# One-pass products of exact parts for the first layer's memory heads, with a softmax turn that starts two chunks earlier

## The chip, the cores and the metric

The kernel runs on one core of one Trainium2 chip, in one launch. The metric is the device time in microseconds of that core. Before the change, three runs took 2043.17, 2043.19 and 2043.20 us; the median is 2043.19 us.

## The reference, cut to what matters

The reference is a two-layer decoder trunk in fp32: 256 positions, model width 2048. Each layer adds a mixer and a gated convolutional MLP. Layer 0 is the one that the change touches. It makes `z = h @ w_in_a` from the normalized input, uses the first 3072 columns for a gated mixer of 12 heads, and the last 512 as queries of four heads that attend to 256 memory tokens:

```python
def memory_attention(q_m, mem, g_mem, w_mem_kv):
    q = q_m.reshape(B, S, MEM_HEADS, MEM_HEAD_DIM)          # 256 x 4 x 128
    kv = rmsnorm(mem, g_mem) @ w_mem_kv
    k = kv[..., :MEM_W].reshape(B, M, MEM_HEADS, MEM_HEAD_DIM)
    v = kv[..., MEM_W:].reshape(B, M, MEM_HEADS, MEM_HEAD_DIM)
    s = jnp.einsum('bshd,bmhd->bhsm', q, k) * (MEM_HEAD_DIM ** -0.5)
    p = jax.nn.softmax(s, axis=-1)
    return jnp.einsum('bhsm,bmhd->bshd', p, v).reshape(B, S, MEM_W)
...
x = x + jnp.concatenate([main, mo], axis=-1) @ w_out[l]
x = x + conv_ffn(rmsnorm(x, g_ffn[l]), w_ffn_up[l], conv_w[l], conv_b[l], w_ffn_down[l])
```

`main` is the gated mixer's 1536 columns (blocks 0 to 11 of 128), `mo` the memory heads' 512 (blocks 12 to 15). Layer 1 has the same memory attention with its own weights; the change leaves it as it is.

## The kernel before, in words

**A product in three passes.** TensorE takes fp32 data in two ways here. A tile of type F32 is multiplied as it is, and a tile of type F32R holds a value that is exact in a shorter form, which takes one pass. The weights are read as fp32, and `chunk` (line 124) makes two F32R tiles of each: ScalarE writes the rounded high part `whi` (L142, or L147 and L164 with a gain), VectorE writes the rest `wlo` (L143, L148). Activations are held in the same way, high part and low part side by side (`xhl`, `mainhl`, `memhl`). A product is then high by high (L179), high weight by low activation (L180) and low weight by high activation (L182): 256 columns each.

**Chunks, pairs and buffers.** A chunk is 128 x 1024 weights, a load of 512 KB that SyncE issues. `raw`, `whi` and `wlo` have four buffers each. `gemm_fm` (line 186) takes two chunks at a time: first L179 and L180 of both, in the order of the chunks, then L182 of both. One pair is 48 matmuls for a GEMM 512 columns wide. `hooks` are functions that are called after a pair, under the number of either chunk.

**What sets the order.** The whole of `start` (line 432) runs under a manual schedule on TensorE, ScalarE, VectorE and SyncE: each engine takes its instructions in the order in which the code is written. In it, the memory's keys and values of layer 0 are accumulated in four PSUM banks over 16 steps, then comes the GEMM of layer 1's keys (eight chunks, `hooks[0]`) and the one of layer 1's values (eight chunks, `hooks[1]`). Layer 0's results are fetched from PSUM by the hooks of the first: under 0 the column scales `mrt`, under 1 the row of scales `mrb` (a matmul, L428, and a copy, L429), under 2 the values `ev` (L477, ScalarE) and the keys `ek` (L260, VectorE), under 3 to 7 the high and low parts of `xhl` (`operand`, L274 and L275). Outside `start` a scheduler sets the order of ScalarE, VectorE and TensorE; in the last two thirds of layer 0's `w_in_a` GEMM SyncE's order is again that of the code.

**Layer 0's memory heads.** In `layer_a` the queries come from a GEMM of eight chunks (`eq` fetches them as F32 `qm`), and then the gated mixer's first half from three GEMMs, c = 0, 1, 2, of eight chunks each. I call their chunks c0.0 to c2.7. Hooks of these three do the memory heads in passing: scores after chunks c0.2 and c0.4 (two heads each, L545, F32), the softmax, then a turn of the probabilities. `Turn.squares` (L91) transposes 32 x 32 squares on VectorE, eight blocks at a time, into `small`; `Turn.place` puts the squares where they belong by 16 DMAs of 64 KB (L96). `self.pending.ask(..., [0] * 6 + [2] * 8)` hands them out: from the call at c = 1, six chunk loads pass, and behind each of the next eight loads SyncE issues two places. The values follow after chunk c2.5 (`out`, L564, F32). `w_out` then starts with blocks 12 to 15, the memory heads.

Of the kernel before, what the change touches and what calls it, by code (L numbers as in the profile page):

```python
# [20 lines left out]
GH = 12  # L21
GW = GH * 128
MH = 4
MW = 512
# [77 lines left out]
class Kernel:  # L102
# [329 lines left out]
    def start(self):  # L432
        nc, t, tc = self.nc, self.t, self.tc
        self.x = self.ap.tile([P, NB, S], F32, name="xT")
        self.xhl = self.ap.tile([P, NB, 512], F32R, tag="xhl", name=self.uid("xhl"))
        mhl = self.ap.tile([P, NB, 512], F32R, tag="big", name=self.uid("memhl"))
        self.kT = [pool.tile([P, MH, S], F32, name=self.uid("kT")) for pool in (self.mk, self.cp)]
        self.mv = [pool.tile([P, 2, MW], F32, name=self.uid("mv")) for pool in (self.mk, self.cp)]
        self.rt = self.cp.tile([P, 2], F32, name="rt0")
        self.rb = self.tmp(self.cp, [P, S], "rbc", 2)  # L440
        with tc.tile_pool(name="st", bufs=1) as st:
            self.gp = st
            mT = st.tile([P, NB, S], F32, name="memT")
            mrt = st.tile([P, 2], F32, name="mrt")
            mrb = st.tile([P, S], F32, name="mrb")
# [16 lines left out]
            kept = {}  # L462
# [8 lines left out]
                self.row_rstd(kept[name], rb, kept[name + "d"])  # L471

            def ek(l, b, acc):
                self.scaled(self.kT[l][:, b : b + 2, :], acc, mrb)

            def ev(l, tb, acc):
                nc.scalar.activation(self.mv[l][:, tb, :], acc, AF.Copy, scale=mrt[:, tb : tb + 1])  # L477

            m = lambda k: mhl[:, k, :]
            w = t["w_mem_kv"]  # L480
# [8 lines left out]
            mm = nc.tensor.matmul  # L489
# [51 lines left out]
    def memory_scores(self, l, h, q, pool, p):  # L541
        nc = self.nc
        acc = self.psum()
        for sb in range(2):
            nc.tensor.matmul(  # L545
                acc[:, sb * S : (sb + 1) * S], q[:, sb * P : (sb + 1) * P], self.kT[l][:, h, :], start=True, stop=True
            )
# [12 lines left out]
    def memory_out(self, l, h, pT, hl):  # L560
        nc, v = self.nc, self.mv[l]
        o = self.psum()
        for mb in range(2):
            nc.tensor.matmul(o[:, :S], v[:, mb, h * P : (h + 1) * P], pT[:, mb * S : (mb + 1) * S], start=mb == 0, stop=mb == 1)  # L564
        self.split(hl[:, GH + h, :], o[:, :S])


# [93 lines left out]
    def layer_a(self):  # L661
# [4 lines left out]
        with ExitStack() as ctx:  # L666
# [20 lines left out]
            qm = la.tile([P, MH, S], F32, name="qm")  # L687
            wT = la.tile([P, GH, P], F32, name="wT")
            bb = la.tile([P, GH, P], F32, name="bb")

            def spatial_weights():
                nc.sync.dma_start(out=bb, in_=t["b_sp"][0].rearrange("(o g) t -> o g t", o=1).to_broadcast([P, GH, P]))
# [14 lines left out]
                        )  # L707

            def eq(b, acc):
                self.scaled(qm[:, b : b + 2, :], acc, rb)  # L710

            hooks = {1: [spatial_weights], **{4 + i: [lambda i=i: gates(3 * i)] for i in range(4)}}
            self.gemm_fm(self.rows(w, 2 * GW, MW), ks, MH, x, eq, hooks=hooks)

            hl = self.ap.tile([P, NB, 512], F32R, tag="big", name=self.uid("mainhl"))
            pm, small = (la.tile([P, MH * 512], F32, name=name) for name in ("pm", "small"))
            turned = Turn(nc, pm, small, 4 * MH)

            def scores(h):
                view = pm[:, 512 * h : 512 * (h + 1)].rearrange("p (m a c) -> p a m c", m=2, a=2)  # L720
                self.memory_scores(0, h, qm[:, h, :], la, view)

            def out(h):
                self.memory_out(0, h, pm[:, 512 * h : 512 * (h + 1)], hl)

            each = lambda f, *hs: [lambda h=h: f(h) for h in hs]
            mhooks = {2: each(scores, 0, 1), 4: each(scores, 2, 3) + [lambda: turned.squares(0, 8)]}, {0: [lambda: turned.squares(8, 8)]}, {5: each(out, *range(MH))}
            for c in range(3):

                def eu(b, acc):  # L730
                    g = 4 * c + b
                    u = self.tmp(la, [P, 2, S], "u", 2)
                    self.scaled(u, acc, rb)
                    nc.scalar.activation(u, u, AF.Gelu)
                    u4 = u.rearrange("p g (n t) -> p g n t", n=2)
                    v4 = vn[:, :, g * P : (g + 2) * P].rearrange("p n (g t) -> p g n t", g=2)
                    nc.vector.tensor_tensor(u4, u4, v4, ALU.mult)
                    self.split_pair(hl[:, g : g + 2, :], u)

                if c == 1:  # L740
                    self.pending.ask(turned.places(), [0] * 6 + [2] * 8)
                with tc.manual_schedule(engines={mybir.EngineType.SP}) if c else nullcontext():
                    self.gemm_fm(self.rows(w, c * 512, 512), ks, 4, x, eu, hooks=mhooks[c])
            self.w_out(0, hl, [12, 13, 14, 15] + list(range(12)))


    def layer_b(self):
# [346 lines left out]
```

## Time and profile before

| | |
|---|---|
| median of three runs | 2043.19 us (2043.17 to 2043.20) |
| span of the profiled execution | 2041.6 us; its own time is not listed apart |
| TensorE busy | 2032.4 us, 100% of the span, 16200 matmul records |
| VectorE, ScalarE busy | 1359.1 us (67%), 1042.8 us (51%) |
| chain that ended last | TensorE 99% |
| granted TensorE clock | 0.999 of full speed on average |
| HBM read | 387.88 MB, 191 GB/s over the span |

The span runs from the first to the last instruction of the profile; the three runs are 1.6 us longer than it. In the rows below, times are microseconds from the span's start. A row of the engines in order of time gives its start, its length, engine, line, operation, output and inputs, and in brackets the idle time ahead of it with what ended it; rows that follow each other on one line are merged (x16). A matmul's length holds its way through the array, so the distance of starts tells its cost. The profile shows an F32 matmul of 256 columns as two records.

### The profile page before, as it was taken

To read this page: it belongs to the slowest core of one execution; us is meant where nothing else is said; L and a number is where in the kernel's file an instruction comes from. 1 tells how busy PE (TensorE), PEld (TensorE's weight loads), DVE (VectorE), ACT (ScalarE), POOL (GpSimd) and SP (SyncE) were. 2 spreads that over 40 slices of the span, in tenths; PEclk is the share of its full clock that TensorE was granted. 3 is DMA by queue.
4 is the path that set the end of the run, shared out by engine and by line. 5 is a ranking of instruction groups with operands and counts; after the bars stand their busy time and mean duration, and the time that the engine had idled before them with its cause. 6 is when DMAs were issued, how large, how long until landed. Compare 5 with 4: busy or idle time off the path is not lost.

```text
span 2041.6 us, 38976 instructions
## 1 busy us (share of the span) xinstructions
PE 2032.4 (100%) x16200; PEld 1966.1 (96%) x16200; DVE 1359.1 (67%) x1847; ACT 1042.8 (51%) x1351; POOL 94.4 (5%) x125
## 2 busy tenths in 40 slices
PE   9999999999999999999999999999999999999998
PEld 8989999999999999999999999999988999889997
DVE  6866667767556666457689876777655667656675
ACT  6754644555435554345555674455543555434543
POOL 0000013000000000000052001200000000000000
PEclk9999999999999999999999999999999999999999
DMA  8575755666656666566665674578766666666654
GB/s 310 189 227 175 196 182 186 201 192 192 199 189 193 198 195 197 188 196 192 190 196 177 177 153 157 189 207 217 223 197 194 190 201 189 195 196 187 197 186 154
DMA packets 236753, 396.70 MB, mean 194 GB/s; under 512 B 47776, under 2 KB 54304, under 8 KB 236448
## 3 DMA queue, kind: packets, MB, share of 16 engines
q1 hardware_dynamic: 236288, 393.70, 63.4%
q8 instruction: 126, 2.06, 0.4%
q10 hardware_dynamic: 288, 0.52, 0.1%
q14 instruction: 51, 0.42, 0.1%
HBM read 387.88 MB, written 2.10 MB: 191 GB/s over the span
## 4 chain that ended last, share of the span: by engine, by line
PE 99%; DMA 0%; issue 0%; DVE 0%; ACT 0%; POOLq 0%; POOL 0%
PE ps L182 26%; PE ps L179 26%; PE ps L180 26%; PE ps L210 6%; PE ps L212 6%; PE ps L211 6%; DMA raw<-in_w_mem_kv 0%; PE ps L877 0%; PE ps L545 0%; PE ps L564 0%; PE ps L517 0%; PE ps L516 0%; PE ps L519 0%; PE ps L703 0%; PE ps L910 0%; PE ps L879 0%
## 5 line engine op out<-in xcount | busy, mean ns | idle before, releaser
L143 DVE TENSOR_TENSOR wlo<-raw,whi 128x1024 fp32r<-128x1024 f32 (+1 forms) x672 | 819.4, 1236 | 607.0 <-issue 402.1
L142 ACT ACTIVATE whi<-raw 128x1024 fp32r<-128x1024 f32 (+1 forms) x672 | 705.0, 1056 | 790.5 <-PE ps L180 579.2
L179 PE MATMUL ps<-xhl,whi 128*128 128x256 f32 x3264 | 752.1, 277 | 0.0
L180 PE MATMUL ps<-xhl,whi 128*128 128x256 f32 x3264 | 750.2, 276 | 0.0
L179 PEld LDWEIGHTS ps<-xhl,whi 128*128 128x128 f32 x3264 | 612.8, 188 | 0.3
L180 PEld LDWEIGHTS ps<-xhl,whi 128*128 128x128 f32 x3264 | 612.6, 188 | 0.3
L182 PE MATMUL ps<-xhl,wlo 128*128 128x256 f32 x3264 | 403.2, 276 | 0.0
L182 PEld LDWEIGHTS ps<-xhl,wlo 128*128 128x128 f32 x3264 | 385.1, 188 | 0.0
L179 PE MATMUL ps<-h,whi 128*128 128x256 f32 x704 | 161.6, 276 | 0.0
L180 PE MATMUL ps<-h,whi 128*128 128x256 f32 x704 | 161.5, 276 | 0.0
L619 DVE SCALAR_TENSOR_TENSOR c<-a,cT,c 128x255 f32<-128x255 f32 (+1 forms) x352 | 146.5, 480 | 0.0
L211 PE MATMUL ps<-wlo,h 128*128 128x512 f32 (+1 forms) x364 | 139.0, 382 | 0.0
L212 PE MATMUL ps<-whi,h 128*128 128x512 f32 (+1 forms) x364 | 138.7, 382 | 0.0
L210 PE MATMUL ps<-whi,h 128*128 128x512 f32 (+1 forms) x364 | 138.3, 382 | 0.0
L179 PEld LDWEIGHTS ps<-h,whi 128*128 128x128 f32 x704 | 132.0, 188 | 0.0
L180 PEld LDWEIGHTS ps<-h,whi 128*128 128x128 f32 x704 | 131.9, 188 | 0.0
L616 ACT ACTIVATE c<-a,cT 128x256 f32<-128x256 f32 x176 | 91.6, 591 | 77.2 <-DVE a L260 77.2
L179 PE MATMUL ps<-mainhl,whi 128*128 128x256 f32 x512 | 118.2, 277 | 0.0
L180 PE MATMUL ps<-mainhl,whi 128*128 128x256 f32 x512 | 117.8, 277 | 0.0
L179 PEld LDWEIGHTS ps<-mainhl,whi 128*128 128x128 f32 x512 | 95.9, 188 | 0.1
L180 PEld LDWEIGHTS ps<-mainhl,whi 128*128 128x128 f32 x512 | 95.8, 188 | 0.1
L182 PE MATMUL ps<-h,wlo 128*128 128x256 f32 x704 | 86.9, 276 | 0.0
(250 smaller groups left out, 1963.2 us busy)
## 6 DMA issues: line engine op xcount, KB each, us to landing
raw<-in_w_ffn_up SPq DMA_DIRECT2D x352, 512.0 KB, 4.2
raw<-in_w_ffn_down SPq DMA_DIRECT2D x176, 512.0 KB, 4.8
raw<-in_w_out SPq DMA_DIRECT2D x64, 512.0 KB, 4.9
raw<-in_w_in_a SPq DMA_DIRECT2D x56, 512.0 KB, 4.4
raw<-in_w_mem_kv SPq DMA_DIRECT2D x30, 512.0 KB, 5.0
raw<-in_w_in_b SPq DMA_DIRECT2D x16, 512.0 KB, 4.5
raw<-in_w_uq SPq DMA_DIRECT2D x12, 384.0 KB, 3.5
raw<-in_w_kv_a SPq DMA_DIRECT2D x8, 512.0 KB, 3.8
```

The source lines that it names most:

```text
L142: nc.scalar.activation(hi[:, :n], raw[:, :n], AF.Copy)
L143: nc.vector.tensor_tensor(lo[:, :n], raw[:, :n], hi[:, :n].bitcast(F32), ALU.subtract)
L179: mm(acc, wh, x[:, :S], start=first, stop=False)
L180: mm(acc, wh, x[:, S:], start=False, stop=False)
L182: mm(acc, wl, x[:, :S], start=False, stop=last)
L210: mm(acc, xh, wh, start=first, stop=False)
L211: mm(acc, xh, wl, start=False, stop=False)
L212: mm(acc, xl, wh, start=False, stop=last)
L616: nc.scalar.activation(c[:, i, :], a[:, i, :], AF.Identity, scale=w(2), bias=w(3))
L619: nc.vector.scalar_tensor_tensor(o, a[:, i, : S - 2 + j], w(j), o, ALU.mult, ALU.add)
```

## The change

- Layer 0's keys `kT[0]` and values `mv[0]` are held as F32R high and low parts. `ek` and `ev` write them for l = 0: `ek` scales the keys into a single fp32 buffer `k0` (VectorE, L260) and splits that (`split_pair`: ScalarE L269, VectorE L270), twice; `ev` writes the high part on ScalarE (L487) and the rest on VectorE (L488). Both still stand under hook 2 of layer 1's key GEMM.
- The queries `qm` are split in the same way by `eq`.
- A score product of 128 queries by 256 keys becomes three F32R matmuls in place of one F32 matmul, and so does each value product.
- `places` are asked with `[0] * 4 + [2] * 8`: two chunks earlier. After chunk c2.3 `parts` makes the high and low parts of the turned probabilities (two ScalarE and two VectorE operations of 128 x 1024), and `out` moves from after chunk c2.5 to after chunk c2.7.
- `w_out` takes the memory heads' blocks 12 to 15 after blocks 0 to 7.
- Tiles share buffers: `turned` is first the spatial weights `wT`, then the probabilities `pm`; `square` is first `bb`, then `small`, then the probabilities' high part; `qm`'s buffer later holds their low part.

```diff
@@ start
-        self.kT = [pool.tile([P, MH, S], F32, name=self.uid("kT")) for pool in (self.mk, self.cp)]
-        self.mv = [pool.tile([P, 2, MW], F32, name=self.uid("mv")) for pool in (self.mk, self.cp)]
+        self.kT = [self.mk.tile([P, MH, 2 * S], F32R, name="kT0"), self.cp.tile([P, MH, S], F32, name="kT1")]
+        self.mv = [self.mk.tile([P, 2, 2, MW], F32R, name="mv0"), self.cp.tile([P, 2, MW], F32, name="mv1")]
...
             def ek(l, b, acc):
-                self.scaled(self.kT[l][:, b : b + 2, :], acc, mrb)
+                if l == 1:
+                    self.scaled(self.kT[1][:, b : b + 2, :], acc, mrb)
+                    return
+                k = self.tmp(st, [P, 2, S], "k0", 1)
+                self.scaled(k, acc, mrb)
+                self.split_pair(self.kT[0][:, b : b + 2, :], k)
 
             def ev(l, tb, acc):
-                nc.scalar.activation(self.mv[l][:, tb, :], acc, AF.Copy, scale=mrt[:, tb : tb + 1])
+                r = mrt[:, tb : tb + 1]
+                if l == 1:
+                    nc.scalar.activation(self.mv[1][:, tb, :], acc, AF.Copy, scale=r)
+                    return
+                hi, lo = self.mv[0][:, tb, 0, :], self.mv[0][:, tb, 1, :]
+                nc.scalar.activation(hi, acc, AF.Copy, scale=r)
+                nc.vector.scalar_tensor_tensor(lo, acc, r, hi.bitcast(F32), ALU.mult, ALU.subtract)
@@ memory_scores
+            qh, ql = q[:, cols], q[:, S + sb * P : S + (sb + 1) * P]
+            mm(o, qh, k[:, :S], start=True, stop=False)
+            mm(o, qh, k[:, S:], start=False, stop=False)
+            mm(o, ql, k[:, :S], start=False, stop=True)
@@ memory_out
+            hi, lo = (x[:, m] for x in pT)
+            mm(o[:, :S], v[:, mb, 0, cols], hi, start=mb == 0, stop=False)
+            mm(o[:, :S], v[:, mb, 0, cols], lo, start=False, stop=False)
+            mm(o[:, :S], v[:, mb, 1, cols], hi, start=False, stop=mb == 1)
@@ layer_a
             def eq(b, acc):
-                self.scaled(qm[:, b : b + 2, :], acc, rb)
+                q = self.tmp(la, [P, 2, S], "u", 2)
+                self.scaled(q, acc, rb)
+                self.split_pair(qm[:, b : b + 2, :], q)
...
+            def parts():
+                ph, pl = (self.tmp(la, [P, MH * 512], tag, 1, F32R) for tag in ("square", "qm"))
+                for h in (0, 2):
+                    cols = slice(512 * h, 512 * (h + 2))
+                    nc.scalar.activation(ph[:, cols], pm[:, cols], AF.Copy)
+                    nc.vector.tensor_tensor(pl[:, cols], pm[:, cols], ph[:, cols].bitcast(F32), ALU.subtract)
+                kept.extend((ph, pl))
...
-            mhooks = {2: each(scores, 0, 1), 4: each(scores, 2, 3) + [lambda: turned.squares(0, 8)]}, {0: [lambda: turned.squares(8, 8)]}, {5: each(out, *range(MH))}
+            mhooks = {2: each(scores, 0, 1), 4: each(scores, 2, 3) + [lambda: turned.squares(0, 8)]}, {0: [lambda: turned.squares(8, 8)]}, {3: [parts], 7: each(out, *range(MH))}
...
-                    self.pending.ask(turned.places(), [0] * 6 + [2] * 8)
+                    self.pending.ask(turned.places(), [0] * 4 + [2] * 8)
...
-            self.w_out(0, hl, [12, 13, 14, 15] + list(range(12)))
+            self.w_out(0, hl, list(range(8)) + [12, 13, 14, 15, 8, 9, 10, 11])
```

What this makes of the order is shown at two places. The first is in `start`, around hook 2 of layer 1's key GEMM. ScalarE before (`whi_643` and `whi_651` are chunks 2 and 3 of that GEMM, `whi_715` and `whi_723` chunks 4 and 5; `mv` the values, `xhl` the high parts of the input):

```order
L147 ACTIVATE whi_651<-raw_650,gT 128x512 x2
L477 ACTIVATE mv_92<-ps_106,mrt 128x512
L477 ACTIVATE mv_92<-ps_107,mrt 128x512
L274 ACTIVATE xhl_88<-xT,gT 128x256 x2
L147 ACTIVATE whi_715<-raw_714,gT 128x512 x2
L147 ACTIVATE whi_723<-raw_722,gT 128x512 x2
```

ScalarE now (chunks 4 and 5 are `whi_723` and `whi_731` here):

```order
L147 ACTIVATE whi_651<-raw_650,gT 128x512 x2
L487 ACTIVATE mv_92<-ps_106,mrt 128x512
L487 ACTIVATE mv_92<-ps_107,mrt 128x512
L269 ACTIVATE kT_90<-k_80_710 128x2x256
L269 ACTIVATE kT_90<-k_81_714 128x2x256
L274 ACTIVATE xhl_88<-xT,gT 128x256 x2
L147 ACTIVATE whi_723<-raw_722,gT 128x512 x2
L147 ACTIVATE whi_731<-raw_730,gT 128x512 x2
```

VectorE at the same place now (`k_80` and `k_81` are the one buffer `k0`; before, only two L260 that wrote `kT` stood between L148 and L275):

```order
L429 COPY mrb<-ps_540 128x256
L148 SCALAR_TENSOR_TENSOR wlo_644<-raw_642,gT,whi_643 128x512 x2
L148 SCALAR_TENSOR_TENSOR wlo_652<-raw_650,gT,whi_651 128x512 x2
L488 SCALAR_TENSOR_TENSOR mv_92<-ps_106,mrt,mv_92 128x512
L488 SCALAR_TENSOR_TENSOR mv_92<-ps_107,mrt,mv_92 128x512
L260 TENSOR_TENSOR k_80_710<-ps_104,mrb 128x512
L270 TENSOR_TENSOR kT_90<-k_80_710,kT_90 128x2x256
L260 TENSOR_TENSOR k_81_714<-ps_105,mrb 128x512
L270 TENSOR_TENSOR kT_90<-k_81_714,kT_90 128x2x256
L275 SCALAR_TENSOR_TENSOR xhl_88<-xT,gT,xhl_88 128x256 x2
```

Two instructions of ScalarE that read `k0` now stand ahead of the high parts of chunks 4 and 5; each needs what VectorE writes behind the copy `mrb` and four L148.

The second place is SyncE's queue in the GEMM c = 1. Before (`raw_2372` to `raw_2440` are the loads of chunks c1.4 to c1.7):

```order
L132 DMA raw_2372<-in_w_in_a 128x2x512
L132 DMA raw_2378<-in_w_in_a 128x2x512
L132 DMA raw_2432<-in_w_in_a 128x2x512
L96 DMA pm<-small 32x16x32 x2
L132 DMA raw_2440<-in_w_in_a 128x2x512
L96 DMA pm<-small 32x16x32 x2
```

SyncE now (`raw_2402` to `raw_2474` are c1.4 to c1.7, `square` is the buffer of `small`, `turned` that of `pm`):

```order
L132 DMA raw_2402<-in_w_in_a 128x2x512
L96 DMA turned_1956<-square_1957 32x16x32 x2
L132 DMA raw_2410<-in_w_in_a 128x2x512
L96 DMA turned_1956<-square_1957 32x16x32 x2
L132 DMA raw_2466<-in_w_in_a 128x2x512
L96 DMA turned_1956<-square_1957 32x16x32 x2
L132 DMA raw_2474<-in_w_in_a 128x2x512
```

The first pair of places now stands ahead of the loads of c1.5 and c1.6, not behind them. On TensorE nothing changes its place but the score and value products.

## Rows read from the trace of the kernel before

**Rows 1.** The page: busy time of TensorE, and the chain that ended last
```profile
PE 2032.4 (100%) x16200; PEld 1966.1 (96%) x16200; DVE 1359.1 (67%) x1847; ACT 1042.8 (51%) x1351; POOL 94.4 (5%) x125
...
PE 99%; DMA 0%; issue 0%; DVE 0%; ACT 0%; POOLq 0%; POOL 0%
```

**Rows 2.** The chain in order of time (start, length): a low-part group, the values
```profile
250.69 1.82 PE ps L182 x16
252.51 3.45 PE ps L564 x16
```

**Rows 3.** TensorE in order of time: the scores of two heads
```profile
199.84 1.89 PE L545 MATMUL ps<-kT,qm 128*128 128x256 f32 x8
```

**Rows 4.** VectorE in order of time, hook 2 of the key GEMM
```profile
57.13 0.42 DVE L429 COPY mrb<-ps 128x256 f32<-128x256 f32 x1 [4.33 <-PE ps L428]
57.48 2.73 DVE L148 SCALAR_TENSOR_TENSOR wlo<-raw,gT,whi 128x512 fp32r<-128x512 f32 x4
60.13 1.28 DVE L260 TENSOR_TENSOR kT<-ps,mrb 128x512 f32<-128x512 f32 x2
```

**Rows 5.** ScalarE in order of time, the same place
```profile
53.86 1.24 ACT L477 ACTIVATE mv<-ps,mrt 128x512 f32<-128x512 f32 x2
55.00 0.90 ACT L274 ACTIVATE xhl<-xT,gT 128x256 fp32r<-128x256 f32 x2
55.80 2.55 ACT L147 ACTIVATE whi<-raw,gT 128x512 fp32r<-128x512 f32 x4
```

**Rows 6.** TensorE in order of time: its first matmul of chunk 4
```profile
62.42 0.28 PE L179 MATMUL ps<-memhl,whi 128*128 128x256 f32 x1
```

**Rows 7.** VectorE and ScalarE in order of time: a split of the same shape
```profile
240.77 1.29 DVE L737 TENSOR_TENSOR u<-u,vn 128x512 f32<-128x512 f32 x2
241.49 0.63 ACT L269 ACTIVATE mainhl<-u 128x512 fp32r<-128x512 f32 x1
242.15 0.69 DVE L270 TENSOR_TENSOR mainhl<-u,mainhl 128x512 fp32r<-128x512 f32 x1
```

**Rows 8.** Busy by stretch: length, PE, PEld, DVE, ACT, POOL, granted clock, DMA
```profile
2032.00:2034.00 2.00, 1.76 (x15) 1.55 (x13) 1.93 (x6) 0.79 (x1) 0.00 (x0) 1.00 0.16 66
2034.00:2036.00 2.00, 0.00 (x0) 0.00 (x0) 1.30 (x5) 0.36 (x1) 0.55 (x1) 1.00 1.00 410
2036.00:2038.00 2.00, 0.00 (x0) 0.00 (x0) 0.79 (x3) 0.98 (x2) 0.00 (x0) 0.55 0.63 236
```

**Rows 9.** TensorE in order of time: F32 matmuls at the start, and later
```profile
1.12 4.46 PE L320 MATMUL ps<-ones 128*128 128x128 f32 x20 [1.12 <-DVE ones L311]
...
178.09 2.84 PE L703 MATMUL ps<-wT,vn 128*128 128x128 f32 x24
```

**Rows 10.** SyncE's queue in order of time, GEMM c = 1
```profile
208.36 6.85 SPq L132 DMA_DIRECT2D raw<-in_w_in_a  x3
218.36 1.41 SPq L96 DMA_DIRECT2D pm<-small  x2
219.81 0.62 SPq L132 DMA_DIRECT2D raw<-in_w_in_a  x1
...
224.08 0.58 SPq L132 DMA_DIRECT2D raw<-in_w_in_a  x1
```

**Rows 11.** VectorE in order of time: the second transpose of the turn
```profile
217.09 1.24 DVE L91 STREAM_TRANSPOSE small<-pm 128x1024 f32<-128x1024 f32 x1
```

**Rows 12.** ScalarE in order of time: high parts of chunks c1.7, c2.1, c2.2
```profile
224.53 1.06 ACT L142 ACTIVATE whi<-raw 128x1024 fp32r<-128x1024 f32 x1 [1.34 <-DMA raw<-in_w_in_a]
...
232.19 1.06 ACT L142 ACTIVATE whi<-raw 128x1024 fp32r<-128x1024 f32 x1 [2.95 <-DMA raw<-in_w_in_a]
236.20 1.06 ACT L142 ACTIVATE whi<-raw 128x1024 fp32r<-128x1024 f32 x1 [2.95 <-PE ps L182]
```

**Rows 13.** TensorE in order of time: first matmuls of chunks c1.6 and c2.0
```profile
230.58 0.28 PE L179 MATMUL ps<-xhl,whi 128*128 128x256 f32 x1
...
236.02 0.28 PE L179 MATMUL ps<-xhl,whi 128*128 128x256 f32 x1
```

More of the change, by code (lines that the diff above doesn't have):

```diff
@@ L543, in memory_scores @@
         acc = self.psum()
+        mm, k = nc.tensor.matmul, self.kT[l][:, h, :]
         for sb in range(2):
-            nc.tensor.matmul(
-                acc[:, sb * S : (sb + 1) * S], q[:, sb * P : (sb + 1) * P], self.kT[l][:, h, :], start=True, stop=True
-            )
+            o, cols = acc[:, sb * S : (sb + 1) * S], slice(sb * P, (sb + 1) * P)
+            if l == 1:
+                mm(o, q[:, cols], k, start=True, stop=True)
+                continue
+            qh, ql = q[:, cols], q[:, S + sb * P : S + (sb + 1) * P]
+            mm(o, qh, k[:, :S], start=True, stop=False)
+            mm(o, qh, k[:, S:], start=False, stop=False)
+            mm(o, ql, k[:, :S], start=False, stop=True)
         scale = 128 ** -0.5
@@ L561, in memory_out @@
         nc, v = self.nc, self.mv[l]
+        mm, cols = nc.tensor.matmul, slice(h * P, (h + 1) * P)
         o = self.psum()
         for mb in range(2):
-            nc.tensor.matmul(o[:, :S], v[:, mb, h * P : (h + 1) * P], pT[:, mb * S : (mb + 1) * S], start=mb == 0, stop=mb == 1)
+            m = slice(mb * S, (mb + 1) * S)
+            if l == 1:
+                mm(o[:, :S], v[:, mb, cols], pT[:, m], start=mb == 0, stop=mb == 1)
+                continue
+            hi, lo = (x[:, m] for x in pT)
+            mm(o[:, :S], v[:, mb, 0, cols], hi, start=mb == 0, stop=False)
+            mm(o[:, :S], v[:, mb, 0, cols], lo, start=False, stop=False)
+            mm(o[:, :S], v[:, mb, 1, cols], hi, start=False, stop=mb == 1)
         self.split(hl[:, GH + h, :], o[:, :S])
@@ L685, in layer_a @@
                 nc.vector.tensor_scalar(vn[:, tb, :], vn[:, tb, :], vr[:, tb : tb + 1], None, ALU.mult)
-            qm = la.tile([P, MH, S], F32, name="qm")
-            wT = la.tile([P, GH, P], F32, name="wT")
-            bb = la.tile([P, GH, P], F32, name="bb")
+            qm = self.tmp(la, [P, MH * 512], "qm", 1, F32R).rearrange("p (h c) -> p h c", h=MH)
+            wT, bb = (self.tmp(la, [P, MH * 512], tag, 1)[:, :GW].rearrange("p (g t) -> p g t", g=GH) for tag in ("turned", "square"))
             def spatial_weights():
@@ L715, in layer_a @@
             hl = self.ap.tile([P, NB, 512], F32R, tag="big", name=self.uid("mainhl"))
-            pm, small = (la.tile([P, MH * 512], F32, name=name) for name in ("pm", "small"))
+            pm, small = (self.tmp(la, [P, MH * 512], tag, 1) for tag in ("turned", "square"))
             turned = Turn(nc, pm, small, 4 * MH)
@@ L721, in scores @@
                 self.memory_scores(0, h, qm[:, h, :], la, view)
+            kept = []
+            def parts():
[5 more added lines that the diff above has]
+                kept.extend((ph, pl))
             def out(h):
-                self.memory_out(0, h, pm[:, 512 * h : 512 * (h + 1)], hl)
+                self.memory_out(0, h, [x[:, 512 * h : 512 * (h + 1)] for x in kept], hl)
             each = lambda f, *hs: [lambda h=h: f(h) for h in hs]
-            mhooks = {2: each(scores, 0, 1), 4: each(scores, 2, 3) + [lambda: turned.squares(0, 8)]}, {0: [lambda: turned.squares(8, 8)]}, {5: each(out, *range(MH))}
+            mhooks = {2: each(scores, 0, 1), 4: each(scores, 2, 3) + [lambda: turned.squares(0, 8)]}, {0: [lambda: turned.squares(8, 8)]}, {3: [parts], 7: each(out, *range(MH))}
             for c in range(3):
```

## The prediction

> **What bounds the kernel now.** I read the page first: busy time, then the chain that ended last [rows 1]. TensorE is busy for 2032.4 of 2041.6 us, and 99% of the chain is its own work. So a matmul that goes is worth its time in full, a pause of TensorE is lost in full, and work on another engine costs nothing until it makes TensorE wait. The question is therefore: what is the matmul work that goes, and at which places does the change make the split of weights (ScalarE, VectorE) or their loads (SyncE) late? For this I read the three other engines in order of time at the two places where the order of instructions changes, against the moment at which TensorE wants the result.
>
> **The matmuls.** The values' 16 records stand in 3.45 us, 0.216 each; 16 one-pass matmuls of 256 columns stand in 1.82 us, 0.114 each [rows 2]. The profile shows an F32 product as two records, and the scores of two heads (four products, eight records) fit the same step: seven steps of 0.216 and a last record of 0.38 make their 1.89 [rows 3]. Layer 0 has eight score and eight value products: 16 x 0.432 = 6.91 us before, 48 x 0.114 = 5.47 after. That takes away 1.45 us, 0.74 of it in the scores. I see no reason for more than 0.1 either way: the new matmuls have the form of the 16 in the row.
>
> **The ladder in `start`.** This is the largest term. ScalarE now has to write the high part of layer 0's keys twice before it may split chunk 4 of layer 1's key GEMM, and each of the two waits for VectorE. VectorE stands at the copy of `mrb`, which waits for TensorE until 57.13, and then does four L148 of chunks 2 and 3 until 60.13 [rows 4]. Before, ScalarE was not bound by this: it had gone on from the values at 53.86 to the split of chunks 4 and 5 at 55.80, on which nothing of VectorE weighed [rows 5]. Now, step by step:
> - two L488 of the L148's form and step (2.65/4 = 0.66): VectorE reaches the first L260 at 61.45 and ends it, 0.68 later, at 62.13;
> - the hand-over is read from a split of the same shape: L269 starts 0.04 after the 0.69 us operation ahead of it ends, takes 0.63, and L270 follows 0.03 later [rows 7]. So the first L269 is at 62.17 to 62.80, L270 at 62.83 to 63.52;
> - `k0` is one buffer, so the second L260 stands behind that: 63.45 to 64.13, and the second L269 at 64.17 to 64.80;
> - ScalarE then does two L274 (0.80) and two L147 (0.61 each by their step) [rows 5]: the first half of chunk 4 is there at about 66.2, the second at 66.85.
>
> TensorE wants chunk 4 at 62.42 [rows 6]. It gets its first two matmuls (0.23) at 66.25 and the rest from 66.9 on: 66.9 - 62.42 - 0.23 = 4.25 us lost. Behind that nothing is late: chunk 5 follows 1.2 us later on ScalarE and is wanted 1.8 us later, the low parts are wanted 3.6 us after the restart and VectorE needs 2.7. The GEMM of layer 1's values starts from TensorE's own end, so it moves along. L488 and the split from `k0` are not in the trace. With all VectorE steps at the L260's 0.60, ScalarE's at 0.60 and no hand-over time it comes to 3.7; with full lengths and 0.1 per hand-over to 5.0. I take 4.25, as the rows have the same shapes.
>
> **The clock.** Such a pause is not free afterwards. At the end of the trace TensorE stops at 2033.8 (1.76 us busy of the stretch from 2032), and in the stretch from 2036 the granted clock averages 0.55: it fell to half at about 2036.2, some 2.4 us after the last matmul [rows 8]. The pause here is 3.8 us, so I expect it to fall. What half a clock costs can be read at the start: the 20 records of 128 columns take 4.46 us, 0.22 each, while 24 of the same form later take 2.84, 0.12 each [rows 9]. The price lies between 0 and 4.46 - 20 x 0.118 = 2.1 us; I take 1.4, two thirds, since a fall late in the pause may be taken back sooner.
>
> The Trainium skill, "TensorE: Matmul & The Clock Gate", section "Seeing it yourself", shows a trace in which the lower clock came 5.2 us after the last matmul. By that figure a pause of 3.8 us passes without a fall, and the sum loses this term: about 2047.1 in place of 2048.5. The row at the end of this trace has less than half of that figure, and I go by the row; the figure is why the first rival below has a large share.
>
> **The places in SyncE's queue.** The first place waits for the second transpose, which ends at 217.09 + 1.24 = 218.33, and starts at 218.36; ahead of it are three loads from 208.36 on, of chunks c1.4 to c1.6, and behind it from 219.81 one load for every two places [rows 10, 11]. Two chunks earlier, the pair of places stands behind c1.4 alone: c1.5 is issued at 219.81 and not among those three, and the next ones each take the slot that in the trace belongs to the chunk two behind. Their time to ScalarE can be read: the load issued at 219.81 was split at 224.53, the one of 224.08 at 232.19, the next at 236.20, each 1.06 long [rows 10, 12]. So c1.7 would have its high part at 233.25 and c2.0 at 237.26. TensorE wants c1.6 at 230.58, c1.7 half a pair's high part later, at 230.58 + 1.81 = 232.39, and c2.0 at 236.02 [rows 13]; all 0.74 earlier by the shorter scores, 231.65 and 235.28. That makes waits of 1.6 and 0.4 us, and `parts`, whose ScalarE work stands ahead of the split of c2.4 and waits for the last places, may add 0.4: 2.4. Against it stands that the softmax also starts earlier, by the shorter scores and up to a microsecond in all; each 0.1 by which the transpose ends earlier takes 0.1 off. Bounds: 0 if the transpose comes 2 us earlier, 4 if the last places hold ScalarE for longer. I take 1.2.
>
> **What I cost at nothing.** The split of the queries (two ScalarE operations of 0.63, two VectorE ones of 0.69) has two pairs of TensorE work, 2 x 48 x 0.114 = 10.9 us, until the scores want it. `parts` on VectorE stands beside work of an engine that is 67% busy. The value products come 5.4 us later, behind the last pair, and `w_out` begins with blocks that were written long before, so their eviction has two pairs of time. If that cover were gone, each would cost no more than its own 1 to 2 us.
>
> **Sum.** -1.45 + 4.25 + 1.4 + 1.2 = +5.4 us on the span of 2041.6: 2047.0. The runs' median lies 1.6 us above the span, so 2048.5 is forecast for them. A change under 0.2% (4.1 us) can't be told from none here.
>
> **Rivals.**
> - *The ladder alone, not slower within 0.2%.* The clock holds through the pause and the loads stay ahead of TensorE: -1.45 + 4.25 + 0 to 1.2, so 2046.0 to 2047.2, in the middle 2046.5. It decides from the point where TensorE restarts before the granted clock falls. For it: the clock stays at 1.00 for over 2 us after the last matmul [rows 8], and the pause is broken by two matmuls. Against it: the pause is longer than that.
> - *The cover holds, and the gain is kept.* If ScalarE had chunk 4 split before the ladder, only the matmuls would count: 2043.19 - 1.45 = 2041.7, and a little more gain if the earlier placing freed something else. For it: the chunks run four buffers ahead. Against it: in the new order both L269 stand ahead of the split of chunk 4, and an engine takes its instructions in order there.
> - *The queue of loads.* If the places hold up loads for the full two chunks, waits at c1.7, c2.0 and c2.4 add up to 4 us in place of 1.2: 2051.3 with the clock's fall. For it: ScalarE already waited 2.95 us for a load there [rows 12]. Against it: the turn's start also moves earlier.
>
> **How the numbers follow.** Forecast 0.50, ladder alone 0.33, cover 0.08, queue 0.09. The forecast's own range is 2046.8 to 2050.0, so 0.44 of its share is slower by over 0.2% (above 2047.28) and 0.06 within. Of the ladder alone I count 0.21 within, and 0.12 slower, as the queue may cost over 1.2 there too. Of the cover's share 0.06 is within 0.2% and 0.02 faster by more; the queue's 0.09 is slower. That gives faster 0.02, same 0.33, slower 0.65. The range that leaves out the cover and the worst of the queue is 2045.0 to 2050.8.
>
> **What would show it.** In the profile of the changed kernel: a pause of TensorE of 3.7 to 5 us near 62.4 ahead of L179, with the wait put down to ScalarE's L147; on ScalarE two L269 at about 62.2 and 64.2 with VectorE as releaser; matmul steps of about twice 0.114 behind the pause and a granted clock below 1 in that stretch; short waits of TensorE near 236 to 242, ahead of L179 of c1.7 and c2.0, with DMA behind ScalarE's wait; 24 score and 24 value matmuls at 0.114. Wrong would be: no pause near 62 (then the order on ScalarE does not bind as I think), a pause without a slower clock behind it (the first rival), or waits at places that I count as covered.

## Result and profile after

The changed kernel takes 2049.49 us (median of 5 runs, 2048.67 to 2051.07), the kernel before beside it 2043.20 (2043.17 to 2043.96): a ratio of 1.0032, 95% interval 1.0021 to 1.0043, so slower by more than 0.2%. Forecast were 2048.5 and slower. The profiled execution took 2048.67 with a span of 2046.9, against 2041.6 before. The page's first lines, which answer to [rows 1]:

```profile
span 2046.9 us, 39029 instructions
...
PE 2033.3 (99%) x16216; PEld 1967.0 (96%) x16216; DVE 1364.8 (67%) x1855; ACT 1046.3 (51%) x1357; POOL 94.4 (5%) x125
```

TensorE is busy for 0.9 us more, although its products became shorter: part of its work ran at the lower clock. The rest of the 5.3 us is time in which it stood. The waits of TensorE over the whole span (releaser: us in total, times, longest), without that of its first matmul:

```profile
PE ps L179 <- ACT whi L147: 3.8, 1, 3.8
...
PE ps L179 <- ACT whi L164: 0.4, 1, 0.4
PE ps L179 <- ACT whi L142: 0.4, 1, 0.4
```

The first is the ladder in `start`. The second stands near 11.5 us, long before the ladder; it stands in the traces of `e8` (0.2) and `e10` (0.5) as well and is no part of the argument. The third is a weight split in the softmax turn. The chain of waits in order of time (start, length; pieces of 0.1 us and less are left out, but for the second L269) shows the ladder step by step, where the kernel before had [rows 4 to 6]:

```profile
60.33 1.32 DVE mv L488 x2
61.65 0.61 DVE k L260
62.28 0.64 ACT kT L269
62.94 0.70 DVE kT L270
63.67 0.70 DVE k L260
64.39 0.05 ACT kT L269
64.58 0.22 issue
64.93 0.89 ACT xhl L274 x2
65.82 0.62 ACT whi L147
66.49 0.58 PE ps L179
```

The split of chunk 4 (the L147) ends behind two rounds between VectorE and ScalarE, and TensorE starts chunk 4 at 66.49 where it did so at 62.42 [rows 6]. TensorE itself, in order of time:

```profile
61.74 0.96 PE L182 MATMUL ps<-memhl,wlo 128*128 128x256 f32 x7
66.49 0.58 PE L179 MATMUL ps<-memhl,whi 128*128 128x256 f32 x1 [3.79 <-ACT whi L147]
```

The last matmul ahead of the pause ends at 62.70. Behind the pause stand the stretches of 2 us (length, PE, PEld, DVE, ACT, POOL, granted clock, DMA):

```profile
64.00:66.00 2.00, 0.00 (x0) 0.00 (x0) 1.31 (x3) 1.60 (x4) 0.00 (x0) 1.00 0.14 54
66.00:68.00 2.00, 1.51 (x6) 1.40 (x7) 2.00 (x5) 2.00 (x4) 0.00 (x0) 0.53 0.00 0
68.00:70.00 2.00, 2.00 (x13) 2.00 (x13) 2.00 (x5) 2.00 (x6) 0.00 (x0) 0.62 0.41 95
70.00:72.00 2.00, 2.00 (x20) 2.00 (x20) 2.00 (x5) 2.00 (x4) 0.00 (x0) 1.00 0.80 263
```

The granted clock is at its lower level from 66.1 (0.53 over the stretch from 66 means half for all but 0.12 us) to 69.5. A busy stretch at the full clock holds 20 matmuls, the one from 68 holds 13.

The products themselves, on TensorE in order of time: the first and the last of the 12 matmuls of two heads' scores, and of the 24 of the values, in place of [rows 2, 3].

```profile
205.54 0.28 PE L562 MATMUL ps<-kT,qm 128*128 128x256 f32 x1
...
206.84 0.28 PE L564 MATMUL ps<-kT,qm 128*128 128x256 f32 x1
...
263.78 0.29 PE L587 MATMUL ps<-square,mv 128*128 128x256 f32 x1
...
266.48 0.28 PE L589 MATMUL ps<-square,mv 128*128 128x256 f32 x1
```

From starts, one step is (206.84 - 205.54)/11 = 0.118 us for the scores and 2.70/23 = 0.117 for the values.

In the turn, ScalarE in order of time waits for loads ahead of the splits of c1.5 and c1.7, which answer to [rows 12] (the last bracket: idle time before, and what ended it):

```profile
230.05 1.06 ACT L142 ACTIVATE whi<-raw 128x1024 fp32r<-128x1024 f32 x1 [4.28 <-DMA raw<-in_w_in_a]
...
236.89 1.06 ACT L142 ACTIVATE whi<-raw 128x1024 fp32r<-128x1024 f32 x1 [2.53 <-DMA raw<-in_w_in_a]
```

The split at 236.89 ends at 237.95, and TensorE takes up c1.7 at 238.00, 0.66 us after the matmul ahead of it where the step is 0.114. On VectorE and in SyncE's queue stand the second transpose of the turn and what follows it, against [rows 10, 11]:

```profile
222.15 1.24 DVE L91 STREAM_TRANSPOSE square<-turned 128x1024 f32<-128x1024 f32 x1
...
223.46 1.42 SPq L96 DMA_DIRECT2D turned<-square  x2
224.93 0.61 SPq L132 DMA_DIRECT2D raw<-in_w_in_a  x1
```

### The profile page after: what moved, and what is told of

Same layout as the page of the kernel before. It is cut to its first block, busy times and chain, and to the rows that moved or that the text cites. A ratio compares the mean times of both kernels' runs of the same rounds, so it can differ in the third digit from the quotient of the medians.

```text
span 2046.9 us, 39029 instructions
## 1 busy us (share of the span) xinstructions
PE 2033.3 (99%) x16216; PEld 1967.0 (96%) x16216; DVE 1364.8 (67%) x1855; ACT 1046.3 (51%) x1357; POOL 94.4 (5%) x125
## 4 chain that ended last, share of the span: by engine, by line
PE 98%; DMA 1%; DVE 0%; ACT 0%; issue 0%; SPq 0%; POOLq 0%; POOL 0%; ACTq 0%; DVEq 0%
PE ps L179 26%; PE ps L180 26%; PE ps L182 26%; PE ps L210 6%; PE ps L212 6%; PE ps L211 6%; DMA raw<-in_w_mem_kv 0%; PE ps L913 0%; DMA raw<-in_w_in_a 0%; PE ps L528 0%; PE ps L527 0%; PE ps L530 0%; PE ps L727 0%; PE ps L946 0%; PE ps L915 0%
## 5 line engine op out<-in xcount | busy, mean ns | idle before, releaser
L182 PE MATMUL ps<-xhl,wlo 128*128 128x256 f32 x3264 | 403.2, 276 | 0.0
L182 PEld LDWEIGHTS ps<-xhl,wlo 128*128 128x128 f32 x3264 | 385.1, 188 | 0.0
L182 PE MATMUL ps<-h,wlo 128*128 128x256 f32 x704 | 86.9, 276 | 0.0
```

What stands on the lines that cost most here:

```text
L182: mm(acc, wl, x[:, :S], start=False, stop=last)
```

## Experiments

Kernels of one group ran on one chip beside the kernel before. That one had a median of 2043.25 us beside the runs of `e1` to `e5`, 2043.31 beside `e6` to `e9`, and 2043.42 beside `e10` to `e12`. Two more readings are used below. Each run has its mean granted clock on record: kernels whose trace has no low stretch ahead of the end of the kernel have 0.999 there, those whose trace has one have 0.997 or 0.998. (It tells that the clock fell, not where: two runs of `e5`, which has no pause in `start`, have 0.998.) And TensorE's loss in a stretch is read by comparing the start of the same matmul with that in the kernel before. The theory is that of the prediction: ladder, clock, and loads behind the places. The rivals are that the ladder alone makes the difference, or that another part of the turn does.

### The ladder and the clock

**`e8_ladder_only`.** The kernel before, with the ladder's instructions alone; they write tiles that nobody reads.

```
             def ek(l, b, acc):
                 self.scaled(self.kT[l][:, b : b + 2, :], acc, mrb)
+                if l == 0:
+                    self.split_pair(self.tmp(st, [P, 2, 512], "kjunk", 1, F32R), self.kT[0][:, b : b + 2, :])
...
+                if l == 0:
+                    nc.vector.scalar_tensor_tensor(self.tmp(st, [P, 512], "vjunk", 1, F32R), acc, ...)
```

> The kernel before, with only the ladder added: under hook 2 the keys are also split into a spare tile and the values' rest is written to a spare tile, with the instructions and the order of the changed kernel; nothing reads them. Theory (ladder 4.2 us and a fall of the clock behind it): pause of 4.0 to 4.1 us ahead of chunk 4, granted clock 0.5 for 3 to 7 us behind or in it, 2048.6 to 2050.4 us, runs over 1 us apart. Rival (the ladder costs its pause alone): 2047.3 to 2047.5 us.

Measured: 2049.57 us (2048.91 to 2050.54, 6 runs), ratio 1.0031 [1.0019, 1.0043]. TensorE pauses for 3.92 us (63.05 to 66.97), and its clock is low from 67.1 to 70.5; the mean clock is below 0.999 in all six runs. The ladder with what it does to the clock costs 6.3 us, as much as the whole change.

**`e9_ladder_filled`.** The same, with 17 F32 products of ones in the pause, whose result nobody reads.

```
+            def fill():
+                spare = self.psum()
+                for i in range(17):
+                    mm(spare[:, :P], self.ones, self.ones, start=True, stop=True)
...
-                    **{3 + i: [call(operand, i)] for i in range(5)},
+                    3: [fill, call(operand, 0)],
+                    **{3 + i: [call(operand, i)] for i in range(1, 5)},
```

> The same, with 17 F32 matmuls of ones into a spare bank in the pause. Theory: the clock stays at full speed, 2047.3 to 2047.6 us, runs within 0.4 of each other; the difference to the run without them is the price of the clock, 1.3 to 3 us. Rival (the slow matmuls behind the pause are not the clock's): no difference.

Measured: 2047.91 us (2047.36 to 2048.33, 10 runs), ratio 1.0022 [1.0013, 1.0032]. The same stretches as above, in this kernel:

```profile
64.00:66.00 2.00, 2.00 (x20) 2.00 (x20) 1.24 (x3) 1.20 (x3) 0.00 (x0) 1.00 0.20 76
66.00:68.00 2.00, 1.77 (x13) 1.37 (x13) 2.00 (x5) 2.00 (x5) 0.00 (x0) 1.00 0.00 0
68.00:70.00 2.00, 2.00 (x20) 2.00 (x19) 2.00 (x5) 2.00 (x6) 0.00 (x0) 1.00 0.14 41
```

The filled pause keeps the clock at 1.00. So the lower clock is worth 2049.57 - 2047.91 = 1.66 us, and the bare ladder 2047.91 - 2043.31 = 4.60; the runs of the two kernels do not overlap. `e8` lies in its range and `e9` 0.3 above its own; the spread of 1.0 us is more than the 0.4 named.

**`e2_filled_pause`.** The changed kernel with the same 17 products.

```
+                    3: [fill, call(operand, 0)],
```

> The changed kernel with 17 F32 matmuls of ones into a spare bank, behind chunks 2 and 3 of layer 1's key GEMM, that is in the pause; they add nothing to the result. Theory (the pause costs 4.2 and the fall of the clock behind it the rest): the pause stays as long, the clock stays at full speed, the step behind it is 0.113 and not 0.21; 2047.0 to 2047.6 us, and the runs lie within 0.5 of each other where the changed kernel's lie over 2.4. Rival (the slow matmuls behind the pause and the spread have another cause): 2048.7 to 2051 us as before.

Measured: 2049.34 us (2047.73 to 2050.43, 6 runs), ratio 1.0029 [1.0018, 1.0041]. The mean clock is 0.999 in all six runs, where the changed kernel's five have 0.997 or 0.998, so the idle products kept the clock. In the profiled run, the fastest (2047.73), TensorE was at chunk 4 at 66.47. But the median missed its range upward and stands level with the changed kernel's: the clock's price did not come back in the time. With the bare ladder at 4.4 and the products at -1.3 (below), 3.0 us are left for the turn (2049.34 - 2043.25 - 4.4 + 1.3). That is a difference and not seen: the kept trace, of the fastest run, loses 0.9 there. `e10` and `e11` repeat it with the turn's waits removed.

**`e3_short_ladder`.** The changed kernel with two buffers for `k0`, and both scaled copies ahead of both splits.

```
-                k = self.tmp(st, [P, 2, S], "k0", 1)
+                k = self.tmp(st, [P, 2, S], "k0", 2)
                 self.scaled(k, acc, mrb)
-                self.split_pair(self.kT[0][:, b : b + 2, :], k)
+                return lambda: self.split_pair(self.kT[0][:, b : b + 2, :], k)
```

> The changed kernel with two buffers k0 and both L260 ahead of both splits, so that the second L269 no longer waits for the first L270. Theory (the length of the pause is the chain of hand-overs): chunk 4's first half is there at about 65.0 and not 66.4, the pause is 2.4 to 2.6 us, 1.4 shorter; with a fall of the clock 2047.3 to 2049, without one 2045.8 to 2046.3. Rival (VectorE's added work sets it, not the hand-overs): the same work, the same pause of 4.06, 2048.7 to 2051 us.

Measured: 2048.48 us (2046.88 to 2051.06, 8 runs), ratio 1.0026 [1.0016, 1.0036]. TensorE goes on at 64.89 in place of 66.49, so 1.6 us of the 4.1 are the single buffer of `k0`, as expected. Its stretches:

```profile
64.00:66.00 2.00, 1.00 (x6) 0.80 (x7) 2.00 (x5) 2.00 (x5) 0.00 (x0) 1.00 0.07 29
66.00:68.00 2.00, 2.00 (x15) 2.00 (x14) 2.00 (x5) 2.00 (x6) 0.00 (x0) 0.68 0.30 52
68.00:70.00 2.00, 2.00 (x11) 2.00 (x10) 2.00 (x6) 2.00 (x4) 0.00 (x0) 0.50 0.83 287
```

In this run the clock was still whole when TensorE resumed, and fell at 66.7, when it had been at work again for 1.8 us. But the profiled run is the slowest of the eight (2051.06). One more (2048.09) has its mean clock of 0.998; the other six have 0.999, so the shorter pause kept the clock in most runs. Without a fall 2045.8 to 2046.3 was expected, and these six took 2046.88 to 2049.40: the median lies in the range named for a fall, but not for that reason. The turn is where the profiled run shows more loss. TensorE waits there four times:

```profile
PE ps L179 <- ACT whi L142: 3.2, 4, 1.4
```

By the starts of its matmuls it loses 4.3 us between 235 and 256, where the changed kernel's profiled run lost 0.9.

### The turn

**`e1_late_split`.** The changed kernel without the ladder: keys and values of layer 0 are kept in F32, and split at the end of `start`.

```
             def ek(l, b, acc):
-                if l == 1:
...
+                self.scaled((k32 if l == 0 else self.kT[1])[:, b : b + 2, :], acc, mrb)
...
             self.gemm_tm(self.rows(w[1], 0, MW), NB, MW, m, lambda tb, acc: ev(1, tb, acc), gain=g, hooks=hooks[1])
+            for b in range(2):
+                self.split_pair(self.kT[0][:, 2 * b : 2 * b + 2, :], k32[:, 2 * b : 2 * b + 2, :])
+            for tb in range(2):
...
```

> The changed kernel with the ladder taken out: hook 2 only fetches layer 0's keys and values in fp32, as before the change (two L260, two ScalarE copies), and the four splits stand at the end of the stage, behind layer 1's values. Theory (two L269 ahead of the split of chunk 4 make the pause, and the pause makes the clock fall): no pause of TensorE near 62, clock at full speed to the end, -1.3 for the matmuls and +0.9 for the waits near 237 stay: 2042.5 to 2043.2 us, runs within 0.3 of each other. Rival (VectorE and ScalarE have too much work in this stage, wherever it stands): the wait moves to 75 to 100 and the time stays above 2046.

Measured: 2044.15 us (2043.13 to 2045.46, 11 runs), ratio 1.0005 [0.9996, 1.0013]. The pause near 62 is gone, and the clock is 1.00 throughout. But the time is 1 us above its range, and its runs 2.3 us apart. Its waits from 215 to 262:

```profile
ACT whi L142 <- DMA raw<-in_w_in_a: 16.3, 7, 4.0
...
PE ps L179 <- ACT whi L142: 1.2, 2, 0.7
```

ScalarE waits for loads for 16 us, up to 4.0 at once, and some of it reaches TensorE: 2.0 us by the starts of its matmuls, in a run that is the median. So a turn term exists without the ladder, and is larger than the profile of the changed kernel showed.

**`e6_places_only`.** The kernel before, with the first two pairs of places two chunks earlier and nothing else.

```
-                    self.pending.ask(turned.places(), [0] * 6 + [2] * 8)
+                    self.pending.ask(turned.places(), [0] * 4 + [2] * 8)
```

> The kernel before, with nothing changed but the places of the turn asked two chunks earlier; F32 heads, no parts. Theory (the places ahead of the loads of c1.5 and c1.6 make weights late): waits of TensorE ahead of L179 between 228 and 250, ScalarE waiting for loads, 0.5 to 2 us: 2043.7 to 2045.2 us, and the runs spread over more than the kernel before's. Rival (only the parts of the probabilities, which stand on ScalarE ahead of the split of c2.4, make TensorE wait): 2043.2 us, no waits.

Measured: 2045.29 us (2044.23 to 2046.81, 11 runs), ratio 1.0010 [1.0001, 1.0019]: 2.0 above the kernel before, its median just over the top of the range that was expected. ScalarE in order of time:

```profile
225.18 1.06 ACT L142 ACTIVATE whi<-raw 128x1024 fp32r<-128x1024 f32 x1 [3.67 <-DMA raw<-in_w_in_a]
```

and SyncE's queue there, against [rows 10]:

```profile
208.58 0.37 SPq L132 DMA_DIRECT2D raw<-in_w_in_a  x1
...
218.58 1.43 SPq L96 DMA_DIRECT2D pm<-small  x2
220.05 0.63 SPq L132 DMA_DIRECT2D raw<-in_w_in_a  x1
```

One load stands ahead of the places in place of three; the next is issued at 220.05 and is split only at 225.18. One number in a list, with no new instruction, takes 2 us in the median: the loads behind the places are late by themselves. The profiled run is the fastest (2044.23); no wait of TensorE is listed for it there, but the starts of its matmuls lose 0.7 us between 230 and 248.

**`e5_both`.** `e1` with the places back where they were, and `parts` at the hook that then follows them.

```
-            ... {3: [parts], 7: each(out, *range(MH))}
+            ... {5: [parts], 7: each(out, *range(MH))}
...
-                    self.pending.ask(turned.places(), [0] * 4 + [2] * 8)
+                    self.pending.ask(turned.places(), [0] * 6 + [2] * 8)
```

> The kernel without the ladder, and the places of the turn back at two chunks later, with the parts of the probabilities after chunk c2.5 in place of c2.3. Theory (places ahead of two loads make the waits near 237): no wait there, 0.9 less than without the ladder alone, 2041.7 to 2042.1 us, the gain of the matmuls alone. Rival (the waits come from the split of the probabilities): they move to c2.6 and c2.7 and the time is that of the kernel without the ladder.

Measured: 2044.32 us (2043.67 to 2046.04, 11 runs), ratio 1.0006 [0.9997, 1.0015]; the theory's 2041.7 to 2042.1 was missed, and the rival named there had the time right, but not the place: the wait came at c2.4, not at c2.6 and c2.7. ScalarE in order of time, and then the wait of TensorE:

```profile
236.82 1.06 ACT L142 ACTIVATE whi<-raw 128x1024 fp32r<-128x1024 f32 x1 [2.37 <-DMA raw<-in_w_in_a]
244.39 2.01 ACT L752 ACTIVATE square<-turned 128x1024 fp32r<-128x1024 f32 x2 [6.51 <-DMA raw<-in_w_in_a]
246.31 1.13 ACT L767 ACTIVATE u<-u 128x512 f32<-128x512 f32 x2
247.34 1.99 ACT L142 ACTIVATE whi<-raw 128x1024 fp32r<-128x1024 f32 x2
```

```profile
PE ps L179 <- ACT whi L142: 2.1, 1, 2.1
```

ScalarE stands for 6.5 us at L752, the first instruction of `parts`, which needs the last places. The split of c2.4 comes behind it, at 247.34, and TensorE waits for that; its starts lose 2.3 us. (The releaser is given by the name of a weight load, but L752 reads only what the places bring.) So the wait went from the loads to `parts`, and at that hook the two-chunk move of the places is what `parts` needed.

**`e7_late_parts`.** `e1` with the old places, `parts` behind the last weight split of the GEMM, and the value products inside `w_out`, whose blocks then run in order.

```
-            ... {3: [parts], 7: each(out, *range(MH))}
+            ... {7: [parts]}
...
-                    self.pending.ask(turned.places(), [0] * 4 + [2] * 8)
+                    self.pending.ask(turned.places(), [0] * 6 + [2] * 8)
...
-            self.w_out(0, hl, list(range(8)) + [12, 13, 14, 15, 8, 9, 10, 11])
+            self.w_out(0, hl, list(range(NB)), {3: each(out, *range(MH))})
```

The four instructions of `parts` are held in program order as well.

> The kernel without the ladder, the places back at two chunks later, the parts held behind the split of chunk c2.7 on ScalarE and VectorE, the value products after the fourth chunk of w_out, and w_out's blocks in their own order. Theory (lateness of the turn made all that was left): no wait of TensorE between 230 and 262, runs within 0.5 of each other, 2043.2 - 1.3 = 2041.8 to 2042.1 us. Rival (the small transfers of the turn hold up the loads in any order): waits stay and the time is 2043 us or more.

Measured: 2042.07 us (2041.60 to 2042.48, 11 runs), ratio 0.9994 [0.9985, 1.0003], as expected. TensorE has one wait left in the whole span, that of its first matmul:

```profile
PE ps L320 <- DVE ones L311: 1.1, 1, 1.1
```

This is the fastest kernel of the study. By medians it gains 1.24 us on the kernel before, which the interval does not tell from nothing, but its slowest run lies below that kernel's fastest (2042.72, 27 runs). The new products are then left with nothing against them.

### Whether the parts add up

**`e10_ladder_late_parts`, `e11_filled_late_parts`, `e12_after_again`.** `e10` is the changed kernel with the turn of `e7`, and the ladder left in; `e11` is `e10` with the filled pause; `e12` is the changed kernel again.

```
 e10:  the three edits of e7 against the changed kernel
 e11:  e10, and
+                    3: [fill, call(operand, 0)],
```

> The changed kernel with only its turn put right as in the seventh kernel (places two chunks later, the parts behind the last weight split, the value products inside w_out); the ladder in `start` stays. If the difference of the changed kernel is a sum of ladder (4.2 to 4.6), clock (1.4 to 1.7) and matmuls (-1.3), this gives 2043.3 + 4.4 + 1.6 - 1.3 = 2048.0, range 2047.5 to 2048.4, a spread of its runs below 1 us, a pause near 62.5 and the clock at half behind it, and no wait of TensorE between 230 and 260. What the changed kernel has above it is then the turn's price, 1 to 2 us in the median. Rival: the turn costs nothing beside the ladder, since the later start of everything gives the loads time; then this stands level with the changed kernel, within 0.4 us.

> The kernel before this one in the list with 17 F32 products of ones in the pause of `start`, whose result nobody reads. The clock stays at 1.0 through the pause; the ladder is then left with its bare length. From the fourth and fifth terms: 2048.0 - 1.5 = 2046.5, range 2046.1 to 2046.9. Rival: the clock's price was given back elsewhere, as the filled pause of the changed kernel was no faster in its median (2049.34); then 2047.7 to 2048.4.

> The changed kernel unchanged, beside the two others on the same chip: 2049.0 to 2050.0 in the median, a spread of its runs of 2 us or more.

| kernel | median us (range, runs) | ratio to before |
|---|---|---|
| `e12`, the changed kernel | 2050.45 (2049.71 to 2050.96, 5) | 1.0034 [1.0021, 1.0046] |
| `e10`, turn put right | 2048.72 (2047.45 to 2049.24, 9) | 1.0024 [1.0015, 1.0034] |
| `e11`, and the pause filled | 2046.54 (2046.27 to 2047.13, 11) | 1.0015 [1.0006, 1.0024] |

The turn's waits cost 1.73 us, the lower clock 2.18, and 3.12 is left over the kernel before: the bare ladder of 4.2 to 4.6 less the products' 1.3. The rival that the clock's price comes back elsewhere falls: `e11` has its 2046.5. That holds with the turn put right; in the changed kernel itself `e2` did not gain it. `e10` is above its range, and spread by 1.8 us where under 1 was expected; `e12` also lies above its range, and spread by 1.3 where 2 or more were expected. `e10` has no wait in the turn, so what is left to vary is the clock. The runs' means agree: its four runs from 2047.45 to 2047.94 have 0.998, and of the five from 2048.72 to 2049.24 four have 0.997. The stretches of the profiled run:

```profile
64.00:66.00 2.00, 0.00 (x0) 0.00 (x0) 1.31 (x3) 1.60 (x4) 0.00 (x0) 0.87 0.17 67
66.00:68.00 2.00, 1.51 (x6) 1.40 (x7) 2.00 (x5) 2.00 (x4) 0.00 (x0) 0.50 0.00 0
68.00:70.00 2.00, 2.00 (x11) 2.00 (x11) 2.00 (x5) 2.00 (x6) 0.00 (x0) 0.50 0.32 110
70.00:72.00 2.00, 2.00 (x12) 2.00 (x11) 2.00 (x5) 2.00 (x4) 0.00 (x0) 0.50 0.83 287
72.00:74.00 2.00, 2.00 (x18) 2.00 (x18) 2.00 (x5) 2.00 (x6) 0.00 (x0) 0.93 0.51 175
```

In this run (2049.03 us) the clock is low from 65.5 to 72.3, in place of 66.1 to 69.5, after a pause that ended at the same 66.49. With half the speed in that time the price is up to half of 5.8 us, where the changed kernel's profiled run paid half of 3.0.

The waits of TensorE in the turn of `e12`:

```profile
PE ps L179 <- ACT whi L142: 0.9, 3, 0.3
```

Three short waits, where the first profile of the same kernel has one of 0.4; by the starts of the matmuls 1.9 us are lost in place of 0.9. Which loads are late differs from run to run. One run of `e12`, the median, has a mean clock of 0.999, by which its clock held through the pause; at 2050.45 us it was no faster for it.

## Why the prediction was right

**The matmuls: -1.45 predicted, -1.3 measured.** A new product takes 0.117 to 0.118 us, not the 0.114 of [rows 2], so 48 of them save 0.14 us less. From the start of the 20th matmul ahead of them to that of the 20th behind, they save 0.32 in each of the two score steps and 0.67 in the values; `e7` gains 1.24 by medians.

**The ladder: +4.25 predicted, 4.2 measured.** TensorE is 3.95 late at the first half of chunk 4 (66.49 against 62.42, less 0.12 by which this run was late before) and 0.26 more at the second. With the clock held it is 0.5 at the second and 4.45 in all (`e2`; `e11` 4.43): at half clock some of that wait is covered by slow matmuls. Step by step the working held: the first L269 was foreseen at 62.17 and came at 62.28, L147 was to end at 66.2 and ended at 66.44. By medians, `e9` less before gives 4.60 and `e11` less before 3.12 + 1.3 = 4.4.

**The clock: +1.4 predicted (0 to 2.1).** It fell, as the row at the end of the trace had led to expect, and the profiled run lost 1.39 to slow matmuls, or 1.1 beyond the 4.45 of the ladder at full clock. Over runs it is more: 1.66 (`e8` less `e9`) and 2.18 (`e10` less `e11`), which is past the upper bound. The step "two thirds" took a fall late in the pause to be taken back sooner; it was taken back at 69.5 in one run and at 72.3 in another. By the 5.2 us of the example in the Trainium skill, "TensorE: Matmul & The Clock Gate", section "Seeing it yourself", the pause would have passed at the full clock; here the fall came 3.4 us after the last matmul (62.70 to 66.1). The measured delay decides, but it is not one number, and there the prediction had some luck. Its 2.4 us was a single reading; at the ends of the 13 traces the delay is 2.3 (`e10`, `e12`) to 5.0 us (`e3`). The end of `e3`, against [rows 8]:

```profile
2040.00:2042.00 2.00, 1.50 (x13) 1.29 (x11) 1.93 (x7) 0.53 (x1) 0.00 (x0) 1.00 0.30 125
...
2044.00:2046.00 2.00, 0.00 (x0) 0.00 (x0) 0.52 (x2) 0.71 (x2) 0.00 (x0) 1.00 0.64 239
2046.00:2048.00 2.00, 0.00 (x0) 0.00 (x0) 0.00 (x0) 0.00 (x0) 0.00 (x0) 0.62 0.78 286
```

The last matmul ends at 2041.5, and the clock falls at 2046.5. A pause of 3.8 us lies inside that spread: the mean clock shows a fall in 24 of the 25 unfilled runs with such a pause (changed kernel, `e8`, `e10`, `e12`), and in two of eight with one of 2.3 (`e3`). "The ladder alone" fell: the clock held in only one run of ten of the changed kernel, and the loads did not stay ahead. Its 2046.5 is the time of `e11`, where the pause is filled and the turn put right.

**The places: +1.2 predicted (0 to 4), 0.9 in the profiled run, 1.7 to 2.1 by three pairs of medians** (`e12` less `e10`, `e6` less before, `e1` less `e7`), and 3.0 and 3.7 by what the medians of `e2` and `e3` have above ladder and products. The mechanism is that of the prediction: the wait at c1.7 is there (0.7 us by the starts), and 0.2 more at c2.4, behind `parts`. The wait at c2.0 is not. It was worked out from the split at 236.20 as if that had waited for a load, but [rows 12] put its wait down to TensorE (L182). By medians the term was undersized: the second transpose ended at 223.39, 5.06 later than before, where TensorE ahead of the scores was 5.70 later. So the softmax came 0.64 earlier against TensorE's time ahead of the scores, the gain of the scores and not the microsecond that was allowed for. That it varies was not foreseen at all: single runs of `e1` lie 2.3 us apart, while those of `e7` with the old places lie 0.9 apart.

**What was costed at nothing.** The queries' split and the order of `w_out`, which is a change of TensorE's order too, show no wait in the profile after. `parts` was given 0.4 in the places' term; at a hook where its places are late it costs 2.3 (`e5`, by its trace, and by its median against that of `e7`). The moved places prevent that, at about the same price.

**The sum.** -1.3 + 4.2 + 1.4 + 0.9 = +5.2 for the profiled run, whose span rose by 5.3. By medians on one chip it is -1.3 + 4.4 + 2.2 + 1.7 = +7.0. That sum has to come out, since its terms are the steps from `e12` to `e10` to `e11` to the kernel before; what tests it is that the -1.3 of `e7` and the ladder of `e9` come from other kernels. Of the 5.4 that was predicted (with which the median is 2048.6 and not 2048.5), the ladder held and the two terms given by a fraction of their bounds were low in most runs. "The cover holds" failed as argued: the two L269 stand ahead of the split. "The queue of loads", at 4 us, was reached in a single trace (`e3`), and not in the medians of the changed kernel.

What stays open: why the loads land at different times from run to run, and why the turn costs more in `e2` and `e3`, whose clock mostly held, than in the changed kernel. No run here separates the DMA engines' order from the arrival of the places' small packets.

## What to carry to other kernels

Where one engine is busy all the time, look for where new work on another engine stands in that engine's order: six short instructions at the wrong hook cost 4.4 us here, at the end of the same stage nothing (`e7`). A pause of the matmul engine of a few us can be paid for twice, and a few idle products in it keep the clock; they gave the time back here only where nothing else was late (`e9`, `e11`, not `e2`). Before a transfer is moved ahead, look for what else stands in its queue. Keep an instruction that waits for it behind the work that does not.

## What the hardware showed

- The clock fell while TensorE was at work again: 1.8 us after the end of a pause of 2.3 us (profiled run of `e3`), to half for 3.4 us. Two of the eight runs of `e3` show a fall in their mean clock.
- From the last matmul of the kernel to the fall of the clock it took between 2.3 us (`e10`, `e12`) and 5.0 us (`e3`) in 13 traces.
- After pauses that ended at the same 66.49, the clock was back at 69.5 in one profiled run and at 72.3 in another; the runs of `e10` lie 1.8 us apart, with no wait in the turn in the trace that was kept.
- One-pass products with new operands in the scores and values ran at 0.117 to 0.118 us where the large GEMMs run at 0.114.
